# Second attention of a two-layer decoder: probabilities copied by transfers into float32r tiles, and transposed from there in three groups by query block

## The chip, the cores and the metric

The kernel runs on one core of one Trainium2 chip. The metric is the time of one execution in microseconds (us) on the device. TensorE (PE in the profile) multiplies and transposes, with its weight loads in a row of their own (PEld); VectorE is DVE, ScalarE is ACT, GpSimd is POOL; SP issues transfers and computes nothing.

## The reference

Two layers of a decoder on a sequence of 512 tokens with 1024 features. Layer 0 mixes tokens by stick-breaking attention, layer 1 by a sparse attention with 16 heads over a shared latent of 128; each is followed by a gated MLP. The change is in the sparse attention, the "second attention":

```python
def block(args):                       # one block of 128 queries
    ...
    _, sel = lax.top_k(isc, topk)      # an indexer picks 128 keys per query
    logits = jnp.einsum('bqhd,bqkd->bqhk', qb, kg) * scale
    logits = logits + jnp.swapaxes(bias, -1, -2).astype(jnp.float32)
    logits = jnp.where(valid[:, :, None, :], logits, NEG)
    p = jax.nn.softmax(logits, axis=-1)
    return jnp.einsum('bqhk,bqkd->bqhd', p, vg)
```

All arithmetic is in float32. The kernel computes the logits of all causal keys and adds a mask, so the 512 by 512 matrix of a head is cut into four query blocks `j` of 128 rows, block `j` having `(j + 1) * 128` keys: ten tiles of 128 by 128 per head.

## The kernel before, in words

Large products are made in three float32r products of a high and a low part (lines 694 to 696). In the second attention one loop runs over the heads `h`, and it is written as a software pipeline: while head `h` is transposed, head `n = h + 1` gets its logits and its softmax. The program order of each engine follows the written code; every engine, and the SP queue, takes its instructions in that order.

- `masked_bias(h, j)` writes the bias and the mask of a query block into a tile `L{j}` (two buffers for each `j`), by POOL for `j` below 2 and by ACT and POOL above (lines 2193 to 2205).
- `logits(n, j)` is three matmuls into a bank `z` (lines 1925 to 1927). `softmax(n, j)` adds the logits to the tile and finds the maximum, on DVE (line 1937). `expo(n, j)` makes the exponentials in place, with their sum, on ACT (line 2224). The division by the sum comes later, on the output.
- `transposed(h, pi, by_act)` turns the ten tiles of a head on PE, each by one transposing matmul with the identity into a PSUM bank `tr` (line 2234), in three groups `pi` of 4, 4 and 2, ordered by key block: group 0 holds key block 0 of all four query blocks, so it needs all four `expo` of the head. ACT copies group 0 out (line 2239), DVE groups 1 and 2 (line 2241), into a tile `pT`.
- `weighted(h)` multiplies `pT` of a pair of heads with the values, once in two heads, at the even ones (line 2265).
- `fill` puts in matmuls of other work: the last query projections (`pt_q`) and the first half of the output projection (`pt_o`), two, one or two lots per head at most.

In an iteration the order on PE is: `logits(n, 0)`, `logits(n, 1)`, at even `h` from 2 on `weighted(h - 2)`, group 0 of head `h`, `fill`, `logits(n, 2)`, group 1, `logits(n, 3)`, at odd `h` `pair_values`, group 2, `fill`. So between the logits of the third query block of a head and group 0 of the same head there stands one end of an iteration and one beginning.

The SP queue carries, in that stage, the bias rows `th` (line 1916), weights `raw` (line 613), and for each pair of heads the sums: `rvd` to memory (line 2276), and back, spread over the partitions, `bs` (line 2282, which waits until `rvd` has landed).

Of the kernel before, what the change touches and what calls it, by code (L numbers as in the profile page):

```python
# [9 lines left out]
F32 = mybir.dt.float32  # L10
F32R = mybir.dt.float32r
BF = mybir.dt.bfloat16
AF = mybir.ActivationFunctionType
OP = mybir.AluOpType
# [5 lines left out]
S = 512  # L20
P = 128
KT = D // P
QT = S // P
# [4 lines left out]
HEADS = 16  # L28
# [16 lines left out]
TRP = [[(0, 0)], [(1, 0), (3, 384)], [(2, 0)]]  # L45
TRW = [512, 512, 256]
LOFF = [0, 128, 384, 768]
LW = 1280
TRO = [0, 512, 1024]

C_ID, C_CAUSAL = 0, 128
C_W = 256
C_LEFT = LW - P
# [520 lines left out]
def kernel_body(ctx, tc, xT, wst, cst, smalls, crow, ccol, relb, outT):  # L574
    nc = tc.nc
    act, dve, pe, pool = nc.scalar, nc.vector, nc.tensor, nc.gpsimd

    cpool = ctx.enter_context(tc.tile_pool(name="cpool", bufs=1))
# [10 lines left out]
        return banks.tile(shape, F32, name=name, tag=tag, bufs=nbanks[tag])  # L589

    sm = cpool.tile([P, S_W], F32, name="sm")
    cons = cpool.tile([P, C_W], F32, name="cons")
    ident = cons[:, C_ID:C_ID + P]
    ones_r = cpool.tile([P, P], F32R, name="ones_r")
    ones_mean = ones_r.bitcast(F32)
    dve.memset(ones_mean, 1.0 / D)
# [355 lines left out]
    def stick_layer(l):  # L952
        with ExitStack() as st:
            man = ExitStack()
            man.enter_context(tc.manual_schedule())
            ap = st.enter_context(tc.tile_pool(name="att_a", bufs=2))
            head = ap.tile([P, 288], F32, name="head", tag="kz00", bufs=1)
            diag = ap.tile([P, LW], F32, name="diag", bufs=1)
# [211 lines left out]
            for k in range(3):  # L1170
                first_part(1, k)
            shift_dot(4)
            nc.sync.dma_start(cons, cst[:, C_LEFT:])
            load_ada(6)
            next(s4)
            fetch(5)
# [30 lines left out]
            for b in range(2):  # L1207
                for e in range(2):
                    pool.memset(kz[b][e][64 - 64 * e:128 - 64 * e].bitcast(F32), 0.0)
            mz = [ap.tile([P, LW], F32, name=f"mz{b}", bufs=1) for b in range(2)]  # L1210
            az = [ap.tile([P, LW], F32, name="a") for _ in range(2)]
            for b in range(2):
                for j in range(QT):
                    c = LOFF[j] + (j + 1) * P
# [599 lines left out]
    def dsa_layer(l, first, man):  # L1814
        with ExitStack() as st:
# [126 lines left out]
            with ExitStack() as si:  # L1942
# [22 lines left out]
                for j in range(1, QT):  # L1965
                    work[j] = ip.tile([P, (j + 1) * P], F32, name=f"work{j}")
                    pool.memset(work[j][:, :j * P], 0.0)
                    pool.tensor_copy(work[j][:, j * P:], cons[:, C_CAUSAL:C_CAUSAL + P])

                def lat_squares():  # L1970
                    ptl = ptile([P, S], "pt_latT", "tr")
# [54 lines left out]

                ptq = ptile([P, S], "pt_qi", "mm")
                drain(project_steps(ptq, chunk(("qi", 3), 0)))
                dve.tensor_scalar(maskb[:, :P], cons[:, C_CAUSAL:C_CAUSAL + P], -1.0, None, op0=OP.mult)
                ptw = ptile([P, S], "pt_w", "tr")  # L2030
                for j in range(QT):
                    pe.transpose(ptw[:, j * P:(j + 1) * P], kw[:, j * P:(j + 1) * P], ident)
# [89 lines left out]
            with ExitStack() as sa:  # L2122
# [70 lines left out]
                def masked_bias(h, j):  # L2193

                    ns = (j + 1) * P
                    c = h * QT + j
                    Ls[h, j] = ap.tile([P, ns], F32, name=f"L{j}")
                    L, b = Ls[h, j], ths[h][:, :ns][:, ::-1]
                    if h == 1:
                        dve.tensor_scalar(L, b, irq[:, c:c + 1], None, op0=OP.mult)  # L2200
                    elif h and j < 2:
                        pool.tensor_scalar(L, b, irq[:, c:c + 1], None, op0=OP.mult)
                    else:
                        act.activation(L, b, AF.Copy, scale=irq[:, c:c + 1])
                    pool.tensor_add(L, L, maskb[:, LOFF[j]:LOFF[j] + ns])
# [16 lines left out]
                def expo(h, j):  # L2222
                    nm, sum_ = heads[h][:2]
                    act.activation(Ls[h, j], Ls[h, j], AF.Exp, bias=nm[:, j:j + 1], scale=-1.0, accum_out=sum_[:, j:j + 1])

                trs = {}

                def transposed(h, pi, by_act):
                    tr = ptile([P, S], "tr", "tr")
                    w = TRW[pi]  # L2230
                    for i, c0 in TRP[pi]:
                        for j in range(i, QT):
                            c = c0 + (j - i) * P
                            pe.transpose(tr[:, c:c + P], Ls[h, j][:, i * P:(i + 1) * P], ident)  # L2234
                    if pi == 0:
                        trs[h] = ap.tile([P, LW], F32, name="pT", bufs=2)
                    t = trs[h][:, TRO[pi]:TRO[pi] + w]
                    if by_act:
                        act.activation(t, tr[:, :w], AF.Copy)
                    else:  # L2240
                        dve.tensor_copy(t, tr[:, :w])

                vals = {}

# [9 lines left out]
                def weighted(h):  # L2254

                    av = pair["av"] = ptile([P, S], "av", "mm")
                    ts = [trs.pop(h + e) for e in range(2)]
                    vs = vals.pop(h)
                    for pi in range(3):
                        for i, c0 in TRP[pi]:  # L2260
                            n = S - i * P
                            c = TRO[pi] + c0
                            for e in range(2):
                                hc = i * P + 64 * e
                                pe.matmul(av[64 * e:64 * e + 64, i * P:], lhsT=vs[:, hc:hc + 64],
                                          rhs=ts[e][:, c:c + n], start=i == 0, stop=pi == 2)

                def pair_sums(rv):
                    rvb = ap.tile([P, QT, 2, 64], F32, name="rvb", tag="bs")
# [47 lines left out]
                for j in range(QT):  # L2317
                    if j:
                        logits(0, j)
                    fill(1)  # L2320
                    if j:
                        softmax(0, j)
                    expo(0, j)
                    if j % 2 == 0:
                        masked_bias(1, j // 2)
                    if j == 0:
                        group_columns(2)
# [13 lines left out]
                for h in range(HEADS):  # L2341
                    n = h + 1
                    more = n < HEADS
                    values = h % 2 == 0 and h > 0
                    if more:
                        begin(n)
                        for j in range(2):
                            logits(n, j)
                        softmax(n, 0)
                        expo(n, 0)  # L2350
                    if values:
                        weighted(h - 2)
                    fill(LATE_STEPS[h][0])
                    transposed(h, 0, True)
                    if more:
                        softmax(n, 1)
                        expo(n, 1)
                        sums(h)
                    else:
                        rvb = sums(h)  # L2360
                        pair_values(h - 1)
                    follow(dve)
                    if h == 3:
                        q_newton(8, EARLY_Q)
                    if h == HEADS - 2:
                        late_dots(2)
                    if not more:
                        late_dots(1)
                    if h + 2 < HEADS:
                        masked_bias(h + 2, 0)  # L2370
                    fill(LATE_STEPS[h][1])
                    if h == 10:
                        follow(dve, 1)
                    if more:
                        logits(n, 2)
                        softmax(n, 2)
                        expo(n, 2)
                    transposed(h, 1, False)
                    if "row" in pair:
                        pair_rows()  # L2380
                    if h + 2 < HEADS:
                        masked_bias(h + 2, 1)
                    if h == 10:
                        follow(dve)
                    if more:
                        logits(n, 3)
                        softmax(n, 3)
                        expo(n, 3)
                    if h % 2 and more:
                        pair_values(h - 1)  # L2390
                    transposed(h, 2, False)
                    if h + 2 < HEADS:
                        for j in range(2, QT):
                            masked_bias(h + 2, j)
                    if n + 3 < HEADS:
                        load_bias(n + 3)
                    if h == 1:
                        q_seed(8, EARLY_Q)
                    if values:
                        pair_hi()  # L2400
                    elif h > 1:
                        pair_lo()
                    fill(LATE_STEPS[h][2])
                    follow(act)
                    if h == HEADS - 4:
                        load_dots(3)
                        bias_job(2, "col")
                    if h == 7:
                        follow(dve)
                    if not more:  # L2410
                        pair_scale(rvb)
# [140 lines left out]
```

## Time and profile before

| what | value |
|---|---|
| time, median of the runs | 1212.46 us |
| the profiled execution: time | 1212.47 us |
| the profiled execution: span of the core | 1210.7 us |
| time around the span | 1.8 us |
| second attention, first to last transpose of line 2234 | 723.7 to about 834 us |

The span is the time from the first to the last instruction on the core. In the rows below a timeline row gives start, duration, engine, line, operation, output and inputs with their shapes; "x4" says that four like instructions were merged in one row. In the rows of transfers the last number is the median time from issue to landing. A tile's buffer numbers are left out.

### The profile page before, as it was taken

To read this page: it belongs to the slowest core of one execution; us is meant where nothing else is said; L and a number is where in the kernel's file an instruction comes from. 1 tells how busy PE (TensorE), PEld (TensorE's weight loads), DVE (VectorE), ACT (ScalarE), POOL (GpSimd) and SP (SyncE) were. 2 spreads that over 40 slices of the span, in tenths; PEclk is the share of its full clock that TensorE was granted. 3 is DMA by queue.
4 is the path that set the end of the run, shared out by engine and by line. 5 is a ranking of instruction groups with operands and counts; after the bars stand their busy time and mean duration, and the time that the engine had idled before them with its cause. 6 is when DMAs were issued, how large, how long until landed. Compare 5 with 4: busy or idle time off the path is not lost.

```text
span 1210.7 us, 18277 instructions
## 1 busy us (share of the span) xinstructions
PE 1204.2 (99%) x6532; PEld 1009.1 (83%) x6532; DVE 1024.2 (85%) x1736; ACT 800.0 (66%) x1366; POOL 243.5 (20%) x282
## 2 busy tenths in 40 slices
PE   9999999999999999999999999999999999999998
PEld 6888788788898998998888777777888888888887
DVE  5898888998989988999788995668989898889883
ACT  5588787368666676765657357774786677677660
POOL 0001100001111111211000357784012122112110
PEclk9999999999999999999999999999999999999999
DMA  9778897629789898896520242245499888788662
GB/s 377 249 205 231 224 244 240 209 87 220 192 217 277 230 245 217 225 290 174 183 70 18 70 140 57 84 137 167 137 234 212 225 190 204 182 184 190 155 147 87
DMA packets 79923, 224.89 MB, mean 186 GB/s; under 512 B 16588, under 2 KB 17356, under 8 KB 79832
## 3 DMA queue, kind: packets, MB, share of 16 engines
q1 hardware_dynamic: 59616, 169.16, 42.3%
q0 software_dynamic: 20192, 54.54, 25.5%
q8 instruction: 51, 0.84, 0.3%
q14 instruction: 40, 0.33, 0.1%
q10 hardware_dynamic: 24, 0.02, 0.0%
HBM read 212.62 MB, written 2.16 MB: 177 GB/s over the span
## 4 chain that ended last, share of the span: by engine, by line
PE 98%; DMA 1%; ACT 0%; DVE 0%; issue 0%; SPq 0%
PE pt_d L1741 16%; PE pt_a L1653 8%; PE pt_u L1622 6%; PE pt_a L1649 6%; PE pt_d L1653 4%; PE pt_u L1626 3%; PE pt_d L1649 3%; PE pt_q L694 2%; PE pt_q L696 2%; PE pt_l L694 2%; PE pt_q L695 2%; PE pt_l L695 2%; PE pt_l L696 2%; PE pt_qk L694 2%; PE pt_qk L696 2%; PE pt_qk L695 2%
## 5 line engine op out<-in xcount | busy, mean ns | idle before, releaser
L1741 PE MATMUL pt_d<-actlo,dnhi 128*128 128x512 f32 x288 | 112.8, 392 | 0.0
L1741 PE MATMUL pt_d<-acthi,dnhi 128*128 128x512 f32 x288 | 112.8, 392 | 0.0
L1531 ACT ACTIVATE whi<-raw 128x1024 fp32r<-128x1024 f32 x72 | 75.8, 1054 | 29.6 <-PE pt_a L1653 13.1
L644 ACT ACTIVATE whi<-raw 128x1024 fp32r<-128x1024 f32 x80 | 84.2, 1052 | 3.6 <-issue 1.1
L1622 PE MATMUL pt_u<-hh,whi 128*128 128x512 f32 x320 | 75.8, 389 | 0.0
L1741 PE MATMUL pt_d<-acthi,dnlo 128*128 128x512 f32 x288 | 73.5, 391 | 0.0
L662 POOL DMA_DIRECT2D wlo<-wst x23 | 19.9, 866 | 265.2 <-DVE hh L806 114.1
L1622 PEld LDWEIGHTS pt_u<-hh,whi 128*128 128x128 f32 x320 | 60.0, 188 | 12.6 <-issue 0.2
L1543 POOL DMA_DIRECT2D wlo<-wst x37 | 32.0, 865 | 167.1 <-ACT wlo L1539 91.4
L1741 PEld LDWEIGHTS pt_d<-actlo,dnhi 128*128 128x128 f32 x288 | 54.3, 188 | 10.1
L1741 PEld LDWEIGHTS pt_d<-acthi,dnhi 128*128 128x128 f32 x288 | 54.2, 188 | 10.1
L1741 PEld LDWEIGHTS pt_d<-acthi,dnlo 128*128 128x128 f32 x288 | 53.1, 188 | 10.3
L653 POOL TENSOR_TENSOR wlo<-raw,whi 128x1024 fp32r<-128x1024 f32 x18 | 44.2, 2456 | 85.7 <-PE pt_q L695 45.8
L1649 PE MATMUL pt_a<-hh,whi 128*128 128x512 f32 x228 | 61.3, 391 | 0.0
L1349 DVE TENSOR_TENSOR_SCAN mz<-mz,diag 128x768 f32<-128x768 f32 (+1 forms) x32 | 47.6, 1487 | 15.2 <-ACT mz L1343 15.0
L722 DVE SCALAR_TENSOR_TENSOR raw<-raw,cond 128x1024 f32<-128x1024 f32 x46 | 57.3, 1273 | 1.4 <-ACT cond L1167 1.3
L1653 PE MATMUL pt_a<-hh,wlo 128*128 128x256 f32 x360 | 57.4, 282 | 0.0
L1653 PEld LDWEIGHTS pt_a<-hh,wlo 128*128 128x128 f32 x360 | 53.1, 190 | 4.5
L1937 DVE CUSTOM_DVE_ANT_0 L<-z,L,cols 128x128 f32<-128x128 f32 (+3 forms) x60 | 32.3, 546 | 28.7 <-PE tr L2234 20.7
L1554 POOL DMA_DIRECT2D whi<-wst x30 | 26.0, 866 | 132.8 <-ACT whi L1551 82.6
L694 PE MATMUL pt_q<-hh,whi 128*128 128x512 f32 x128 | 51.8, 405 | 0.0
L722 DVE SCALAR_TENSOR_TENSOR ada<-ada,cond 128x1024 f32<-128x1024 f32 x41 | 50.0, 1219 | 1.7 <-DMA ada<-wst 1.7
(409 smaller groups left out, 3803.3 us busy)
## 6 DMA issues: line engine op xcount, KB each, us to landing
raw<-wst SPq DMA_DIRECT2D x215, 512.0 KB, 5.2
wlo<-wst POOLq DMA_DIRECT2D x60, 512.0 KB, 7.8
ada<-wst SPq DMA_DIRECT2D x45, 512.0 KB, 5.4
raw<-wst SPq DMA_DIRECT2D x48, 384.0 KB, 4.8
whi<-wst POOLq DMA_DIRECT2D x30, 256.0 KB, 5.8
dnlo<-wst POOLq DMA_DIRECT2D x16, 384.0 KB, 7.0
x<-xt POOLq DMA_DIRECT2D x18, 256.0 KB, 5.6
th<-relb SPq DMA_DIRECT2D x16, 256.0 KB, 4.0
```

Of the source, the lines that this page charges most:

```text
L644: act.activation(hi[:, :n], raw[:, :n], AF.Copy)
L653: engine.tensor_sub(lo[:, :w], raw[:, :w], hi[:, :w].bitcast(F32))
L694: pe.matmul(out, lhsT=whi, rhs=ahi, start=start, stop=False)
L695: pe.matmul(out, lhsT=wlo, rhs=ahi, start=False, stop=False)
L696: pe.matmul(out, lhsT=whi, rhs=alo, start=False, stop=stop)
L722: dve.scalar_tensor_tensor(raw, raw, 1.0, cond, op0=OP.mult, op1=OP.mult, accum_out=dst)
L1349: dve.tensor_tensor_scan(rev, rev, diag[:, b:e][:, ::-1], 0.0, OP.mult, OP.max)
L1531: act.activation(W[j, i][0], R[j, i], AF.Copy)
L1622: pe.matmul(pt[j, i], lhsT=W[j, i][0][:, k * P:(k + 1) * P], rhs=hs[k][n], start=k + n == 0, stop=False)
L1649: pe.matmul(pt[j, bank, "both"], lhsT=w[:, c0 + k * P:c0 + (k + 1) * P], rhs=a[2], start=new and k == 0, stop=False, skip_group_check=True)
L1653: pe.matmul(out, lhsT=w[:, c0 + k * P:c0 + (k + 1) * P], rhs=a[n], start=new and k + n == 0, stop=part == 1 and k == 3 and what in ("a2", ...
L1741: pe.matmul(pt["dn", i], lhsT=dn[i][part][:, k * P:(k + 1) * P], rhs=A[j0 + k][n], start=part + k + n == 0, stop=part == 1 and k == j1 - j ...
```

## The change

For heads 0 to 14, a transfer on the SP queue copies the exponentials into tiles `ra` (query blocks 0 to 2, 768 columns) and `rb` (query block 3, 512 columns), one buffer each, which are of type float32r; the bytes are copied as they are. The tiles `L0`, `L1`, `L2` become one tile `La`, so that one transfer moves three query blocks (head 0 is moved in four pieces). PE transposes from the copies, as float32r with a float32r identity. The groups are now by query block: the first two take three tiles each of query blocks 0 to 2, the third the four tiles of query block 3. `pT` is written in strided slots, and `weighted` reads it so. Head 15 is transposed from its own tiles as before, in the new groups. The identity is made once by POOL from `diag`, and serves all float32 transposes through a view of the same bytes; `cons` keeps the causal mask only.

```diff
+SLOTS = [slice(0, 7, 2), slice(3, 8, 2), slice(1, 9, 7), slice(9, 10)]
+TURNS = [([(0, 0), (0, 1), (0, 2)], slice(0, 5, 2)), ([(2, 2), (1, 1), (1, 2)], slice(1, 6, 2)),
+         ([(0, 3), (1, 3), (2, 3), (3, 3)], slice(6, 10))]
...
-    ident = cons[:, C_ID:C_ID + P]
+    ident_r = cpool.tile([P, P], F32R, name="ident_r")
+    ident = ident_r.bitcast(F32)
...
+            pool.tensor_copy(ident_r, diag[:, :P])
...
-                    Ls[h, j] = ap.tile([P, ns], F32, name=f"L{j}")
+                    if j == 0:
+                        Ls[h] = ap.tile([P, LOFF[3]], F32, name="La")
+                    Ls[h, j] = Ls[h][:, LOFF[j]:LOFF[j] + ns] if j < 3 else ap.tile([P, ns], F32, name="Lb")
...
+                def move(h, js):
+                    for j in js:
+                        if j == 0:
+                            moved[h, 0] = ap.tile([P, LOFF[3]], F32R, name="ra", bufs=1)
+                        if j == 3:
+                            moved[h, 1] = ap.tile([P, S], F32R, name="rb", bufs=1)
+                    if h and 0 in js:
+                        nc.sync.dma_start(moved[h, 0].bitcast(F32), Ls[h])
+                    elif h:
+                        nc.sync.dma_start(moved[h, 1].bitcast(F32), Ls[h, 3])
...
-                    for i, c0 in TRP[pi]:
-                        for j in range(i, QT):
-                            c = c0 + (j - i) * P
-                            pe.transpose(tr[:, c:c + P], Ls[h, j][:, i * P:(i + 1) * P], ident)
+                    blocks, slots = TURNS[pi]
+                    for n, (i, j) in enumerate(blocks):
+                        c, k = slice(n * P, n * P + P), slice(i * P, i * P + P)
+                        if h == HEADS - 1:
+                            pe.transpose(tr[:, c], Ls[h, j][:, k], ident)
+                        else:
+                            src = moved[h, 1] if j == 3 else moved[h, 0][:, LOFF[j]:]
+                            pe.transpose(tr[:, c].bitcast(F32R), src[:, k], ident_r)
...
                     transposed(h, 1, False)
+                    if n < HEADS - 1:
+                        move(n, [0, 1, 2])
...
                     transposed(h, 2, False)
+                    if n < HEADS - 1:
+                        move(n, [3])
```

Three places show how the instructions stand. First the SP queue around heads 3 and 4; `th` is a bias row, `rvd` and `bs` the sums out and back, `raw` a chunk of weights. Before:

```order
L1916 DMA th<-relb 128x512 x2
L2276 DMA rvd<-rv 128x2x4
L2282 DMA bs<-rvd 64x512 x2
L1916 DMA th<-relb 128x512
L613 DMA raw<-wst 128x1024
```

And with the change, over the same stretch:

```order
L1921 DMA th<-relb 128x512
L2245 DMA ra<-La 128x768
L2247 DMA rb<-Lb 128x512
L1921 DMA th<-relb 128x512
L2302 DMA rvd<-rv 128x2x4
L2245 DMA ra<-La 128x768
L2308 DMA bs<-rvd 64x512 x2
L2247 DMA rb<-Lb 128x512
L1921 DMA th<-relb 128x512
L617 DMA raw<-wst 128x1024
```

At head 3 the two copies stand between two bias rows; at head 4 the copy `ra` stands ahead of the transfer `bs`, and `rb` behind it. The second place is the SP queue in the iteration of heads 12 and 13, where three chunks of weights stand (`shd` is a small row for a later bias). Before:

```order
L1916 DMA th<-relb 128x512
L613 DMA raw<-wst 128x1024 x3
L710 DMA shd_8460<-mod_88 128x8
L2276 DMA rvd<-rv 128x2x4
L2282 DMA bs<-rvd 64x512 x2
L613 DMA raw<-wst 128x1024 x3
```

And with the change:

```order
L1921 DMA th<-relb 128x512
L2245 DMA ra<-La 128x768
L2247 DMA rb<-Lb 128x512
L617 DMA raw<-wst 128x1024 x3
L714 DMA shd_8492<-mod_89 128x8
L2302 DMA rvd<-rv 128x2x4
L2245 DMA ra<-La 128x768
L2308 DMA bs<-rvd 64x512 x2
L2247 DMA rb<-Lb 128x512
L617 DMA raw<-wst 128x1024 x3
```

The three chunks, which followed the bias row, now stand behind the two copies of head 13. The third place is PE, from the last matmul of the logits of head 3's third query block (width 384) on; the transposes here are those of head 2. Before:

```order
L1927 MATMUL z<-kpl,qh 128x384
L2234 MATMUL tr<-cons,L_7363 128x128
L2234 MATMUL tr<-cons,L_7376 128x128
L2234 MATMUL tr<-cons,L_7379 128x128 x2
L1925 MATMUL z<-kph,qh 128x512
L1926 MATMUL z<-kph,ql 128x512
L1927 MATMUL z<-kpl,qh 128x512
L2234 MATMUL tr<-cons,L_7376 128x128
L2234 MATMUL tr<-cons,L_7379 128x128
L694 MATMUL pt_q<-hh,whi 128x512
```

And with the change:

```order
L1932 MATMUL z<-kpl,qh 128x384
L2263 MATMUL tr<-ident_r,ra 128x128 x3
L1930 MATMUL z<-kph,qh 128x512
L1931 MATMUL z<-kph,ql 128x512
L1932 MATMUL z<-kpl,qh 128x512
L2263 MATMUL tr<-ident_r,rb 128x128 x4
L698 MATMUL pt_q<-hh,whi 128x512
```

The order of the work on PE stays; six transposes in this stretch became seven, and the last four now read `rb`.

More of the change, by code (lines that the diff above doesn't have):

```diff
@@ L591, in kernel_body @@
     sm = cpool.tile([P, S_W], F32, name="sm")
-    cons = cpool.tile([P, C_W], F32, name="cons")
-    ident = cons[:, C_ID:C_ID + P]
+    cons = cpool.tile([P, P], F32, name="cons")
+    ident_r = cpool.tile([P, P], F32R, name="ident_r")
+    ident = ident_r.bitcast(F32)
     ones_r = cpool.tile([P, P], F32R, name="ones_r")
@@ L1172, in stick_layer @@
             shift_dot(4)
-            nc.sync.dma_start(cons, cst[:, C_LEFT:])
+            nc.sync.dma_start(cons, cst[:, C_LEFT + C_CAUSAL:])
             load_ada(6)
@@ L1967, in dsa_layer @@
                     pool.memset(work[j][:, :j * P], 0.0)
-                    pool.tensor_copy(work[j][:, j * P:], cons[:, C_CAUSAL:C_CAUSAL + P])
+                    pool.tensor_copy(work[j][:, j * P:], cons)
                 def lat_squares():
@@ L2028, in dsa_layer @@
                 drain(project_steps(ptq, chunk(("qi", 3), 0)))
-                dve.tensor_scalar(maskb[:, :P], cons[:, C_CAUSAL:C_CAUSAL + P], -1.0, None, op0=OP.mult)
+                dve.tensor_scalar(maskb[:, :P], cons, -1.0, None, op0=OP.mult)
                 ptw = ptile([P, S], "pt_w", "tr")
@@ L2226, in dsa_layer @@
                 trs = {}
+                moved = {}
+                def move(h, js):
[9 more added lines that the diff above has]
+                    else:
+                        for j in js:
+                            ns = (j + 1) * P
+                            to = moved[h, 1] if j == 3 else moved[h, 0][:, LOFF[j]:LOFF[j] + ns]
+                            nc.sync.dma_start(to.bitcast(F32), Ls[h, j])
@@ L2228, in transposed @@
                 def transposed(h, pi, by_act):
                     tr = ptile([P, S], "tr", "tr")
-                    w = TRW[pi]
-                    for i, c0 in TRP[pi]:
-                        for j in range(i, QT):
-                            c = c0 + (j - i) * P
-                            pe.transpose(tr[:, c:c + P], Ls[h, j][:, i * P:(i + 1) * P], ident)
+                    blocks, slots = TURNS[pi]
[3 more added lines that the diff above has]
+                            pe.transpose(tr[:, c], Ls[h, j][:, k], ident)
+                        else:
+                            src = moved[h, 1] if j == 3 else moved[h, 0][:, LOFF[j]:]
+                            pe.transpose(tr[:, c].bitcast(F32R), src[:, k], ident_r)
@@ L2235, in transposed @@
                     if pi == 0:
-                        trs[h] = ap.tile([P, LW], F32, name="pT", bufs=2)
-                    t = trs[h][:, TRO[pi]:TRO[pi] + w]
+                        trs[h] = ap.tile([P, LW], F32, name="pT", bufs=2).rearrange("p (s c) -> p s c", c=P)
+                    t, v = trs[h][:, slots], tr[:, :len(blocks) * P].rearrange("p (s c) -> p s c", c=P)
                     if by_act:
-                        act.activation(t, tr[:, :w], AF.Copy)
+                        act.activation(t, v, AF.Copy)
@@ L2240, in transposed @@
                     else:
-                        dve.tensor_copy(t, tr[:, :w])
+                        dve.tensor_copy(t, v)
                 vals = {}
@@ L2258, in weighted @@
                     vs = vals.pop(h)
[L2259 to L2266, printed above, removed]
+                    for i in (0, 1, 3, 2):
+                        for e in range(2):
+                            hc = i * P + 64 * e
+                            pe.matmul(av[64 * e:64 * e + 64, i * P:].rearrange("p (s c) -> p s c", c=P), lhsT=vs[:, hc:hc + 64],
+                                      rhs=ts[e][:, SLOTS[i]], start=i == 0, stop=i == 2)
                 def pair_sums(rv):
@@ L2323, in dsa_layer @@
                     expo(0, j)
+                    move(0, [j])
                     if j % 2 == 0:
```

## The prediction

> **What bounds the kernel now.** I read the page first, for the engine that sets the end, then the stretches of the second attention, then PE's waits there, and last the timeline of single heads.
>
> ```profile
> span 1210.7 us, 18277 instructions
> PE 1204.2 (99%) x6532; PEld 1009.1 (83%) x6532; DVE 1024.2 (85%) x1736; ACT 800.0 (66%) x1366; POOL 243.5 (20%) x282
> PE 98%; DMA 1%; ACT 0%; DVE 0%; issue 0%; SPq 0%
> sum 120.00, PE 118.81 PEld 94.15 DVE 82.37 ACT 84.58 POOL 87.84; mean PE 9.90 PEld 7.85 DVE 6.86 ACT 7.05 POOL 7.32
> PE av L2265 <- ACT vals L2252: 0.7, 1, 0.7
> PE z L1925 <- DVE nm L1937: 0.4, 1, 0.4
> ```
>
> The second row is the busy time by engine, the third the chain that ended last, the fourth the sum over twelve stretches of 10 us from 720 to 840 us, the last two are all waits that PE has from 720 to 840 us. PE is busy for 1204.2 of 1210.7 us and makes 98% of the chain; in the second attention it is busy for 118.81 of 120 us and waits for others for 1.1 us. So what makes PE's own work in this stage shorter comes off the end, and every new wait of PE is added to it. DVE, ACT and POOL have 32 to 38 us of idle time there. PE takes its work in order, so a transpose that waits holds up all that stands behind it, `fill` too.
>
> **What the transposes cost.** The timeline of PE at group 1 of head 2, and at two narrow logits a little later:
>
> ```profile
> 741.06 0.60 PE L2234 MATMUL tr<-cons,L 128*128 128x128 f32 x4
> 741.42 0.48 PE L1925 MATMUL z<-kph,qh 128*128 128x512 f32 x1
> 741.74 0.39 PE L1926 MATMUL z<-kph,ql 128*128 128x512 f32 x1
> 741.97 0.40 PE L1927 MATMUL z<-kpl,qh 128*128 128x512 f32 x1
> ...
> 743.81 0.22 PE L1925 MATMUL z<-kph,qh 128*128 128x128 f32 x1
> 743.87 0.27 PE L1926 MATMUL z<-kph,ql 128*128 128x128 f32 x1
> 743.98 0.28 PE L1927 MATMUL z<-kpl,qh 128*128 128x128 f32 x1
> 744.09 0.33 PE L1925 MATMUL z<-kph,qh 128*128 128x256 f32 x1
> ```
>
> Durations overlap, so I go by starts. From 741.06 to 741.74 PE does four float32 transposes and one matmul of 512 columns; the next one of 512 columns takes 741.97 - 741.74 = 0.23. The four cost 0.68 - 0.23 = 0.45, that is 0.112 us each. What would a float32r operation of this size cost? The logits of lines 1925 to 1927 are float32r, and at 128 columns the steps are 0.06, 0.11 and 0.11: the first has its weights loaded ahead under a longer matmul, and each one that follows with new weights takes 0.11. A transpose has new weights every time (the probabilities are the stationary operand), so I expect a float32r transpose to step by 0.11 too, as a float32 one does. **150 transposes at 0.112 become 150 at about 0.11: 0 us.** Bounds: at 0.06, if the weights were no limit, 150 x 0.052 = 7.8 us less; on the other side 0.113, the longest such step that I see, nothing that counts. I take 0, since two of the three steps in these rows say so.
>
> A rule of the Trainium skill says otherwise. "TensorE: Matmul & The Clock Gate", section "Weight-path perf modes — Fast Weight Load (FWL) and DoubleRow", has weights of 128 columns loaded faster, about twofold as measured there, when their type is not FP32. If float32r counts as such, the new transposes would come at the lower bound, and the sum would be that of the first rival below. The 0.11 steps of the float32r logits speak against it here.
>
> **What the copies add.** Before, PE reads the exponentials as soon as ACT has made them. Now a transfer stands between, and group 0 of head `n` needs query blocks 0 to 2 of that head. So the gap counts between the end of `expo(n, 2)` on ACT and the first transpose of head `n` on PE, as it is now. Heads in order (each pair: the exponentials of 384 columns, then the first transposes of the same head): 0, 1, 4, 7, 9, 12, 13.
>
> ```profile
> 721.77 0.62 ACT L2224 ACTIVATE Lu<-Lu,cols 128x384 f32<-128x384 f32 x1
> 723.69 0.49 PE L2234 MATMUL tr<-cons,Lu 128*128 128x128 f32 x3
> ...
> 727.13 0.62 ACT L2224 ACTIVATE L<-L,nm 128x384 f32<-128x384 f32 x1 [0.57 <-DVE nm L1937]
> 729.60 0.38 PE L2234 MATMUL tr<-cons,L 128*128 128x128 f32 x2
> ...
> 749.60 0.62 ACT L2224 ACTIVATE L<-L,nm 128x384 f32<-128x384 f32 x1 [0.28 <-DVE nm L1937]
> 754.53 0.33 PE L2234 MATMUL tr<-cons,L 128*128 128x128 f32 x1
> ...
> 771.50 0.62 ACT L2224 ACTIVATE L<-L,nm 128x384 f32<-128x384 f32 x1 [0.91 <-DVE nm L1937]
> 773.28 0.49 PE L2234 MATMUL tr<-cons,L 128*128 128x128 f32 x3
> ...
> 784.48 0.62 ACT L2224 ACTIVATE L<-L,nm 128x384 f32<-128x384 f32 x1 [0.92 <-DVE nm L1937]
> 787.45 0.38 PE L2234 MATMUL tr<-cons,L 128*128 128x128 f32 x2
> ...
> 805.70 0.60 ACT L2224 ACTIVATE L<-L,nm 128x384 f32<-128x384 f32 x1
> 810.00 0.33 PE L2234 MATMUL tr<-cons,L 128*128 128x128 f32 x1
> ...
> 813.39 0.62 ACT L2224 ACTIVATE L<-L,nm 128x384 f32<-128x384 f32 x1 [1.60 <-DVE nm L1937]
> 815.85 0.38 PE L2234 MATMUL tr<-cons,L 128*128 128x128 f32 x2
> ```
>
> Start plus duration of the first row, taken from the start of the second, gives the gap. The odd heads are short: 1.85 at head 1 and 1.84 at head 13, the first and the last of five alike (1, 3, 5, 11, 13); 1.16 at head 7, 2.35 at head 9. The even heads have `weighted` ahead of group 0 and are long: 4.31 at head 4, and the shortest is 3.70 at head 12. Head 0 has 1.30. The new groups add one transpose to the stretch (six became seven), so each gap from head 1 on grows by 0.1.
>
> How long a copy takes no row shows: none here goes from SBUF to SBUF on the SP queue. The nearest rows are these (KB each, median from issue to landing):
>
> ```profile
> raw<-wst SPq DMA_DIRECT2D x48, 384.0 KB, 4.8
> th<-relb SPq DMA_DIRECT2D x16, 256.0 KB, 4.0
> bs<-rvd SPq DMA_DIRECT2D x14, 128.0 KB, 2.9
> outT<-x SPq DMA_DIRECT2D x6, 256.0 KB, 2.0
> outT<-x SPq DMA_DIRECT2D x4, 128.0 KB, 1.7
> ```
>
> `ra` has 384 KB. Read from SBUF as `outT` is, it takes 2.0 + 0.3 = 2.3 (0.3 for another 128 KB); as the loads from memory do, up to 4.8. At 128 KB the transfer that writes SBUF, `bs`, takes 1.2 more than the one that reads it; how much of that is the write, I can't tell. I take 2.8, nearer to `outT`, and keep 2.3 and 4.8 as the ends. To it come 0.1 for ACT to read out its sum before it signals, and 0.1 for PE to start anew (both estimates from the tenth or so between neighbours in these rows): **the first transpose can start 3.0 us after the exponentials.** The Trainium skill, "DMA: Bandwidth & Descriptors", section "Anatomy of one DMA — SWDGE (gpsimd) path", has 2.0 us plus bytes over 436 GB/s; by that `ra` takes 2.9, an estimate, and the sum would be 0.8 us longer. No run so far shows such a copy.
>
> The waits of PE, 3.0 less the gap: heads 1, 3, 5, 11, 13 at 3.0 - 1.95 = 1.05 make 5.25; head 7 at 3.0 - 1.26 makes 1.74; head 9 at 3.0 - 2.45 makes 0.55; head 0, whose last piece is 192 KB (0.45 less than 384 KB, so 2.55 in all), 2.55 - 1.30 = 1.25. The even heads from 2 on have at least 3.8 and wait for nothing. **Sum 8.8 us.** Behind the waiting transpose stand the logits of the next head and `fill`, so nothing covers it; after it everything moves on by the same amount, and the gaps stay as they are, because the way from a logit through DVE and ACT follows PE.
>
> **What I cost at nothing, and what covers it.** `rb` is read by group 2 of its head, a whole iteration of PE's work after it is issued, which hides it; if that were gone, PE would wait for it as for `ra`. The copy-outs of the groups are 3, 3 and 4 tiles, not 4, 4 and 2: the same bytes on ACT and DVE, which have the idle time above. `weighted` has the same sixteen matmuls in another order. `La` comes free when `ra` has landed, which is no later than the transposes that freed `L` before. POOL's copy of the identity falls in a long idle time before the first transposes.
>
> **The SP queue.** It is in order, so a copy waits there for ACT, and what stands behind it waits along.
>
> ```profile
> 810.46 1.38 SPq L613 DMA_DIRECT2D raw<-wst  x3
> ```
>
> The three chunks left at 810.46, ahead of the exponentials of head 13 (done at 814.01); now they stand behind both its copies and leave some 5 us later. Then `rvd`, `ra` of head 14 and `bs` follow close behind 1.5 MB. `bs` waits for `rvd` to land, and `rb` of head 14 stands behind `bs`. Head 14 has a long gap, so I take 0, with 1 us as the upper bound. In the earlier iterations each chunk follows a bias row that already waits for ACT, so it keeps its place.
>
> **Sum:** 1210.7 + 1.8 around the span + 0 + 8.8 = 1221.3, so 1221. The profiled run, 1212.47, and the median, 1212.46, are the same number.
>
> **The rivals.**
>
> *The transposes become cheaper and pay for the waits* (not slower). With 0.06 each, PE saves 7.8; but seven of them lie in the gap, which shrinks by 0.36 at seven odd heads, so 2.5 come back. With my copy: 8.8 + 2.5 - 7.8 = 3.5, time 1216; with a copy of 2.3: 4.8 + 2.5 - 7.8 = -0.5, time 1212. For it speaks the step of 0.06 where weights are loaded ahead; against it, that a row of transposes never has that. The rule on fast weight loads named above (the Trainium skill, "TensorE: Matmul & The Clock Gate") would bring it about. Chance 0.17.
>
> *The copy is as slow as a load* (slower by over 2%). At 4.8 the first transpose starts 5.0 after the exponentials: each of the eight heads waits 2.0 longer than above, 24.8 in all, and the even heads wait too, 1.2 at head 12, 0.6 at head 4 and likewise at two or three more, about 3: time 1240. The point from which this decides is a copy of about 4.5 us, since 2% is 24 us (about what a measurement of this kernel can tell from no change). For it speaks that `raw` and `th` take 4.0 and more; against it, that these read memory and often stand behind others in the queue, while the copies mostly go out alone. Chance 0.07; for a copy from 3.5 to 4.5, which gives 1227 to 1236, another 0.13.
>
> *The copies are hidden after all.* With a landing under 1.7 us only head 7 would wait: time 1213. The shortest row, 1.7 for a third of the bytes, speaks against it. Chance 0.05.
>
> **How the numbers follow.** My forecast (transposes as before, a copy of 2.3 to 3.5, so 1217 to 1227) has 0.58. The range from 1212 to 1233 takes in the rival with cheaper transposes, and most of the slow copies; what is left out is the copy of over 4.2 us (0.1) and a few cases below. Faster by over 2% needs 24 us, more than all the transposes cost (150 x 0.112 = 16.8): 0.01. Slower by over 2%: 0.07. Within: 0.92.
>
> **What the profile after would show.** A new wait of PE at the float32r transposes, put down to the transfers of `ra`, at heads 0 and the odd ones, about 1 us each, and none or little at the even ones. Starts of three transposes 0.11 apart. `ra` from issue to landing about 2.8. No other stage changes. I am wrong if the steps are near 0.06, if the landing is over 4 us, if PE waits at `rb`, or if DVE or ACT become what PE waits for.

## The result, and the profile after

The changed kernel takes 1225.56 us (median; 1225.11 to 1226.19) where the kernel before took 1212.45 beside it: a ratio of 1.0109, with an interval of 1.0089 to 1.0128. It is slower by 13.1 us, which is inside the 2% that counts as no change and inside the range, 4.6 us above the predicted 1221. One of the four runs of the kernel before took 2427.06 us, far from the other three, and the ratio goes without it. The profiled execution took 1225.82 us, with a span of 1224.0 against 1210.7; the 13.3 us between the spans are what has to be explained.

From the page and from the view of transfers of the changed kernel: the span, the busy times, the chain, and the two copies (KB, median from issue to landing).

```profile
span 1224.0 us, 18401 instructions
PE 1206.2 (99%) x6532; PEld 1007.8 (82%) x6532; DVE 1026.6 (84%) x1736; ACT 799.2 (65%) x1366; POOL 243.6 (20%) x283
PE 91%; DMA 2%; DVE 2%; ACT 1%; POOL 1%; issue 1%; SPq 0%; DVEq 0%; POOLq 0%; ACTq 0%
ra<-La SPq DMA_DIRECT2D x14, 384.0 KB, 2.9
rb<-Lb SPq DMA_DIRECT2D x14, 256.0 KB, 2.6
```

PE's busy time grew by 2 us, the span by 13: most of the time is in waits. The chain, which was PE for 98%, now goes over transfers (2%), DVE (2%), ACT and POOL as well. PE's waits from 715 to 855 us, by releaser (total, times, longest); a last one, for a maximum, is 0.3:

```profile
PE tr L2263 <- DMA ra<-La: 8.2, 8, 1.6
PE av L2291 <- DVE pT L2270: 1.8, 1, 1.8
PE tr L2263 <- DMA ra<-Lu: 1.6, 2, 1.2
```

The first and the third row are the wait that was forecast: 9.8 us at the transposes, for the copies into `ra`. Of these 1.2 are at head 10, where none was forecast. There is none for `rb`. The second row, a wait of `weighted(14)` for DVE, was not forecast.

**The gap between exponentials and transposes.** For heads 1, 3 and 4 the exponentials of 384 columns, and the first transposes of the same head:

```profile
729.89 0.62 ACT L2231 ACTIVATE La<-La,nm 128x384 f32<-128x384 f32 x1 [1.77 <-DVE nm L1942]
733.34 0.42 PE L2263 MATMUL tr<-ident_r,ra 128*128 128x128 f32 x3 [0.84 <-DMA ra<-La]
745.53 0.61 ACT L2231 ACTIVATE La<-La,nm 128x384 f32<-128x384 f32 x1 [1.78 <-DVE nm L1942]
749.25 0.43 PE L2263 MATMUL tr<-ident_r,ra 128*128 128x128 f32 x3 [1.13 <-DMA ra<-La]
752.95 0.62 ACT L2231 ACTIVATE La<-La,nm 128x384 f32<-128x384 f32 x1 [0.28 <-DVE nm L1942]
758.21 0.44 PE L2263 MATMUL tr<-ident_r,ra 128*128 128x128 f32 x3
```

Head 1: 733.34 - 730.51 = 2.83. Head 3: 749.25 - 746.14 = 3.11. The other odd heads lie between 2.83 and 2.89. Head 4 has 4.64 and no wait in brackets: the copy is there long before `weighted(2)` is done.

**The transposes.** PE at groups 1 and 2 of head 2:

```profile
744.56 0.38 PE L2263 MATMUL tr<-ident_r,ra 128*128 128x128 f32 x3
744.77 0.46 PE L1930 MATMUL z<-kph,qh 128*128 128x512 f32 x1
745.07 0.39 PE L1931 MATMUL z<-kph,ql 128*128 128x512 f32 x1
...
745.53 0.46 PE L2263 MATMUL tr<-ident_r,rb 128*128 128x128 f32 x4
745.83 0.47 PE L698 MATMUL pt_q<-hh,whi 128*128 128x512 f32 x1
746.13 0.40 PE L699 MATMUL pt_q<-hh,wlo 128*128 128x512 f32 x1
```

By the method of the prediction (start of the group to start of the second matmul behind it, less 0.23): (745.07 - 744.56 - 0.23) / 3 = 0.093, and (746.13 - 745.53 - 0.23) / 4 = 0.093 for a float32r transpose, against 0.112 for a float32 one. 150 of them save 150 x 0.019 = 2.9 us.

**Where the 13.3 us went.** I compared the starts of PE's matmuls in the two traces, which stand in the same order but for a few places. A step in the difference is what was lost there (a minus is a gain); it is a little more than the wait in brackets, since without a wait a matmul starts ahead of the end of the one before it.

| part | forecast, us | in the trace, us |
|---|---|---|
| waits for `ra`, heads 1, 3, 5, 7, 9, 11, 13 | 7.5 | 1.02 + 1.30 + 1.38 + 1.75 + 0.57 + 1.10 + 1.03 = 8.15 |
| waits for `ra`, head 0 | 1.25 | 2.2 |
| wait for `ra`, head 10 | 0 | 1.15 |
| 150 transposes | 0 | -2.9 |
| PE at half clock behind the wait of head 7 | not seen | +1.5 |
| last head: DVE late with `pT` | not seen | +2.8 |
| head 4: the kernel before waits 0.7 for its values at `weighted(2)`, the changed one does not | not seen | -0.8 |
| ahead of the stage, nearly all in a step at 483 us | not seen | +0.8 |
| behind the stage, at 1079 us | not seen | +0.4 |
| sum | 8.8 | 13.3 |

The change does not touch the code at 483 and at 1079 us. Experiment 2, which has no copies, loses 1.1 us at the first of these places, and experiment 7, which has them, nothing at either, so these steps do not come from the copies. The wait at head 4 is gone in experiment 2 as well.

**The half clock.** A view of two neighbouring stretches (busy time of PE, PEld, DVE, ACT, POOL with counts, then the granted clock, the share of the DMA engines, GB/s):

```profile
776.45:779.86 3.41, 1.83 (x15) 1.52 (x13) 3.07 (x10) 2.98 (x8) 3.24 (x6) 1.00 0.58 226
779.86:783.27 3.41, 3.41 (x13) 2.92 (x12) 0.73 (x3) 1.24 (x6) 3.24 (x5) 0.50 0.51 85
```

In the first, PE waits for head 7 and is busy for 1.83 of 3.41 us. In the second it has no gap, but the clock is 0.50: PE gets through thirteen instructions, where experiment 6 has 24 at the same place at full clock. So at most half of the 3.41 us is lost, 1.7; the starts of PE's matmuls on the two sides of the stretch move apart by 1.5 against experiment 6.

**The last head.** The wait for `pT`, in the changed kernel:

```profile
844.84 2.35 POOL L657 TENSOR_TENSOR wlo<-raw,whi 128x1024 fp32r<-128x1024 f32 x1 [6.91 <-ACT whi L648]
844.92 2.29 DVE L730 TENSOR_TENSOR mod<-mod,sm 128x8 f32<-128x8 f32 x1
847.13 1.14 DVE L2270 COPY pT<-tr 128x384 f32<-128x384 f32 x2
848.33 1.94 PE L2291 MATMUL av<-pT,vals 128*64 128x512 f32 x12 [1.75 <-DVE pT L2270]
```

And the same two operations in the kernel before:

```profile
834.57 0.17 DVE L726 TENSOR_TENSOR mod<-mod,sm 128x8 f32<-128x8 f32 x1
834.60 2.38 POOL L653 TENSOR_TENSOR wlo<-raw,whi 128x1024 fp32r<-128x1024 f32 x1 [6.90 <-ACT whi L644]
```

DVE's addition to `mod`, eight columns wide, takes 0.17 us where it starts 0.03 ahead of POOL's large operation on `wlo`, and 2.29 us, until that operation has ended (847.21 and 847.19), where it starts 0.08 behind it. The copies to `pT` stand behind it on DVE, and `weighted(14)` waits for them. PE's matmuls just ahead of `weighted(14)` start 10.2 us later than in the kernel before, those just behind it 13.0, so the last head costs 2.8, more than the 1.75 in brackets.

### The profile page after: what moved, and what is told of

It reads as the page before. It is cut to its first block, busy times and chain, and to the rows that moved or that the text cites. A ratio compares the mean times of both kernels' runs of the same rounds, so it can differ in the third digit from the quotient of the medians.

```text
span 1224.0 us, 18401 instructions
## 1 busy us (share of the span) xinstructions
PE 1206.2 (99%) x6532; PEld 1007.8 (82%) x6532; DVE 1026.6 (84%) x1736; ACT 799.2 (65%) x1366; POOL 243.6 (20%) x283
## 4 chain that ended last, share of the span: by engine, by line
PE 91%; DMA 2%; DVE 2%; ACT 1%; POOL 1%; issue 1%; SPq 0%; DVEq 0%; POOLq 0%; ACTq 0%
PE pt_d L1746 16%; PE pt_a L1658 8%; PE pt_u L1627 6%; PE pt_a L1654 5%; PE pt_d L1658 4%; PE pt_u L1631 3%; PE pt_d L1654 3%; PE pt_l L698 2%; PE pt_l L700 2%; PE pt_l L699 2%; PE pt_qk L698 2%; PE pt_q L698 2%; PE pt_qk L700 2%; PE pt_qk L699 2%; PE pt_q L700 2%; PE pt_q L699 2%
## 5 line engine op out<-in xcount | busy, mean ns | idle before, releaser
L1746 PEld LDWEIGHTS pt_d<-actlo,dnhi 128*128 128x128 f32 x288 | 54.2, 188 | 10.2
L1942 DVE CUSTOM_DVE_ANT_0 La<-z,La,cols 128x128 f32<-128x128 f32 (+2 forms) x45 | 21.1, 481 | 35.1 <-PE z L1932 27.6
```

The costliest lines, as they stand in the source:

```text
L1746: pe.matmul(pt["dn", i], lhsT=dn[i][part][:, k * P:(k + 1) * P], rhs=A[j0 + k][n], start=part + k + n == 0, stop=part == 1 and k == j1 - j ...
```

## Experiments

The theories carry one name each below, beside the letters of the quoted expectations. **Waits:** PE stands still until `ra` has landed, and all else moves on with it. **Clock:** a wait can bring a stretch at half clock. **Tail:** the wait for `pT` is an accident of order between DVE and POOL. The rivals are that the new groups, the strided copies or the extra load on the queue cost the time. The ratios below go by runs of the kernel before that were taken beside each experiment; their medians, 1213.05 us for experiments 1 to 4 and 1212.99 for 5 to 8, lie some 0.6 above the 1212.45 beside the changed kernel, so a difference between two of the times below can be off by about as much.

**1. Copies, but all in float32.** `ra`, `rb` and the transposes are float32; the order is that of the change.

```diff
-    moved[h, 0] = ap.tile([P, LOFF[3]], F32R, name="ra", bufs=1)
+    moved[h, 0] = ap.tile([P, LOFF[3]], F32, name="ra", bufs=1)
...
-    pe.transpose(tr[:, c].bitcast(F32R), src[:, k], ident_r)
+    pe.transpose(tr[:, c], src[:, k], ident)
```

> The kernel with the change, but the copies and their transposes are float32 (same transfers, same groups). Theory A (a float32r transpose steps by 0.093 us, a float32 one by 0.112; the copies' waits are the cost): 150 x 0.019 = 2.9 us more work on PE, of which about 1.1 comes back because the seven transposes in the gap make the waits shorter: about 1227.4 us, waits for ra about 8.5 us. Rival B (the type makes no difference, as the prediction had it): 1225.6 us, waits for ra as with the change, about 9.8 us.

Measured: 1224.38 us (1224.05 to 1225.59), ratio 1.0095 (1.008 to 1.011), span 1222.5. Both expectations are missed on the low side: I had set them out from the time of the changed kernel, and in this run neither the wait for `pT` nor the half clock came. PE's waits for copies:

```profile
PE tr L2263 <- DMA ra<-La: 8.2, 8, 2.0
PE tr L2263 <- DMA ra<-Lu: 1.8, 3, 1.3
```

In all they are again about 10 us, so it is not the type of the copies that makes PE wait. In detail they differ: head 10 alone waits 1.96 here and 1.20 in the changed kernel, and without it the waits are 8.0 against 8.6, which goes the way of theory A, whose slower transposes lengthen the gap. At the last head DVE's addition started at 845.92, 0.04 ahead of POOL's operation, and took 0.17 us again.

**2. The groups alone.** No copies; float32 transposes from `La` and `Lb`, in the new groups and slots.

```diff
-    if h == HEADS - 1:
+    if True:
         pe.transpose(tr[:, c], Ls[h, j][:, k], ident)
...
-    if n < HEADS - 1:
-        move(n, [0, 1, 2])
```

> The kernel with the change without its transfers: float32 transposes straight from La and Lb, in the new groups, with the strided pT. Theory A (the waits for the copies are the cost): no wait of PE at the transposes; what stays is the end of the stage, where weighted waits for DVE's last copy-outs of head 15, 2.3 us: about 1214.8 us. Rival C (the new groups or the strided slots cost it): 1220 us or more. If the late copy-outs are an accident of the copies' timing: 1212.5 us.

Measured: 1211.88 us (1211.38 to 1212.59), ratio 0.9991 (0.9981 to 1.0), span 1210.8. PE's only wait from 715 to 855 us:

```profile
PE z L1930 <- DVE nm L1942: 0.2, 1, 0.2
```

The groups by query block, the strided copies to `pT` and the joined tile `La` cost nothing. Between this kernel and the one of experiment 1 only the copies differ. The times are 12.5 us apart; the starts of PE's matmuls in the two traces part by 11.7, all of it at head 0, the odd heads and head 10, and 10.0 of that are the waits in brackets.

**3. float32r without copies.** ACT writes the exponentials straight into the float32r tiles, in place of having their bytes copied; nothing is moved, and all 160 transposes are float32r. `Lb` and `rb` have one buffer each.

```diff
-    act.activation(Ls[h, j], Ls[h, j], AF.Exp, bias=nm[:, j:j + 1], scale=-1.0, accum_out=sum_[:, j:j + 1])
...
+    to = Rs[h, 1] if j == 3 else Rs[h][:, LOFF[j]:LOFF[j] + (j + 1) * P]
+    act.activation(to, Ls[h, j], AF.Exp, bias=nm[:, j:j + 1], scale=-1.0, accum_out=sum_[:, j:j + 1])
```

> No transfers: ACT writes the exponentials straight into float32r tiles (they are rounded to float32r there, which is the part of the computation that is changed), and all 160 transposes are float32r. One buffer instead of two for Lb and rb. Theory A: 160 x 0.019 = 3.0 us less than the kernel with the groups only: 1211.8 us with the wait at the end of the stage, 1209.5 us without it. Rival B (the type makes no difference): the same time as the kernel with the groups only.

Measured: 1214.63 us (1213.36 to 1217.19), ratio 1.0013 (1.0004 to 1.0022), span 1213.8. The waits for copies are gone, but the kernel is not faster than before. From 720 to 828 us PE gained 2.3 us on the kernel before; then came the wait for `pT`:

```profile
PE av L2276 <- DVE pT L2255: 2.2, 1, 2.2
```

```profile
833.40 2.34 POOL L657 TENSOR_TENSOR wlo<-raw,whi 128x1024 fp32r<-128x1024 f32 x1 [6.91 <-ACT whi L648]
833.49 2.28 DVE L730 TENSOR_TENSOR mod<-mod,sm 128x8 f32<-128x8 f32 x1
```

POOL started 0.09 ahead, DVE's addition took 2.28 us, and behind the wait the clock was at one half from 838.05 on for 3.41 us. So the wait for `pT` does not need the copies. With the half clock it costs 4.8 us here, by the starts of PE's matmuls against experiment 5. Experiment 5 takes it away.

**4. The `fill` ahead of group 0.** Copies as in the change, but at head 0 and the odd heads the matmuls of `fill` that stood behind group 0 go ahead of it, so that PE has work while the copy lands.

```diff
+LATE_STEPS = [(a + b, 0, c) if h % 2 and h < 15 or h == 0 else (a, b, c) for h, (a, b, c) in enumerate(LATE_STEPS)]
```

> The kernel with the change, but at head 0 and the odd heads up to 13 the one or two lots of other matmuls that stood behind group 0 stand ahead of it, which adds 1.4 us (0.7 at head 7) to the gap between the exponentials and group 0. Theory A: with a copy of 2.9 us the waits go at all heads except head 7 (1.0 us left) and head 10 (1.1 us, whose copy stands behind a chunk of weights), and with the wait of 1.6 us at head 7 the stretch of 3.4 us at half the granted clock: 1225.6 - 7.7 - 1.7 - 1.5 (starting anew) = about 1214.7 us. Rival D (PE only waits elsewhere, as the logits that follow are not later but the copies are): 1220 us or more.

Measured: 1217.38 us (1216.42 to 1217.85), ratio 1.0035 (1.0022 to 1.0048), span 1216.1. The first and the second wait in the trace:

```profile
PE tr L2264 <- DMA ra<-La: 1.9, 2, 1.0
PE av L2292 <- DVE pT L2271: 1.7, 1, 1.7
```

8.2 us at eight places became 1.9 at two, and the kernel came out 8.2 us faster than the changed one. The transfers themselves are all still there, so it is PE's standing still that costs, and not the load on the queue. The time is 2.7 above what the first theory gave; the wait for `pT`, again 1.7, and smaller ones for `rb` and for the values, which it left out, are most of that.

**5. As 3, with the last head mended.** At the last head DVE's additions to `mod` (`late_dots(1)`) go behind its copies to `pT`.

```diff
-                    if not more:
-                        late_dots(1)
...
                     transposed(h, 2, False)
+                    if not more:
+                        late_dots(1)
```

> ACT writes the exponentials (rounded to float32r) straight into float32r tiles, no copies; and at the last head DVE's copies to pT stand ahead of its small additions to mod, so that these additions no longer stand between POOL's wlo and pT. The same without the second part took 1214.6, with a wait for pT of 2.2 us and a stretch of 3.4 us at half clock behind it. Theory T (the wait for pT comes from an addition that stalls beside POOL, and the wait brings the half clock): wait for pT gone, no half clock there, 1214.6 - 2.2 - 1.7 = 1210.7 or a little less, 1209.5 to 1211, which is 1 to 3 us under the kernel before. Theory U (float32r exponentials make that wait, whatever the order on DVE): the wait for pT stays above 1.5 us and the time is 1214 to 1215.

Measured: 1210.85 us (1210.65 to 1213.05), ratio 0.9981 (0.9972 to 0.999), span 1208.9. All waits of PE from 715 to 855 us, and the last head:

```profile
PE av L2276 <- ACT vals L2266: 1.0, 2, 0.8
PE z L1930 <- DVE nm L1942: 0.3, 1, 0.3
```

```profile
832.64 3.33 POOL L657 TENSOR_TENSOR wlo<-raw,whi 128x1024 fp32r<-128x1024 f32 x1 [6.92 <-ACT whi L648]
831.47 1.15 DVE L2255 COPY pT<-tr 128x384 f32<-128x384 f32 x2
833.78 2.21 DVE L730 TENSOR_TENSOR mod<-mod,sm 128x8 f32<-128x8 f32 x1
```

The addition still starts inside POOL's operation and still lasts until its end, but nothing that PE needs is behind it. The medians of experiments 3 and 5 lie 3.8 us apart, where 2.2 + 1.7 = 3.9 were expected. That they agree so well is partly luck: the runs of experiment 3 go from 1213.36 to 1217.19, with mean clocks from 0.998 to 1.0, and the two profiled runs are 4.9 apart. This is the version that beats both kernels, by 2.1 us the one before; that is a difference that this measurement shows, though far under 2%. Experiment 2, which has no float32r transposes, is already 1.2 under the runs of before beside it.

**6. The changed kernel with the last head mended.** The same edit on the changed kernel.

> The changed kernel with DVE's copies to pT of the last head ahead of the small additions; the copies by transfers stay. Theory T: the wait for pT (1.8) goes, nothing else changes: 1225.6 - 2.0 = 1223.6, 1223 to 1224.2 where head 7 still brings 3.4 us at half clock, and 1.7 less where it does not. Theory U (the tail's wait belongs to the later arrival of the whole stage and comes back at another place): 1225 to 1226.

Measured: 1224.77 us (1223.3 to 1226.57), ratio 1.0096 (1.0082 to 1.011), span of the profiled run 1222.3. The wait for `pT` is gone from the trace, and the span is 1.7 shorter, though the waits for copies came to 11.3 us here against 9.8 (head 10 waited 2.06). The median moved only by 0.8 and its spread overlaps that of the changed kernel, so by the time alone this stays inconclusive. The spread goes with the clock: the four runs had mean clocks of 0.999 (1223.3 us), 0.998 (1224.1) and 0.997 (1225.44, 1226.57). The profiled run shows where the clock fell, and where not. Two pairs of neighbouring stretches, first around head 7, then around head 0:

```profile
777.67:781.08 3.41, 1.81 (x15) 1.50 (x13) 3.33 (x10) 2.98 (x8) 3.24 (x6) 1.00 0.59 230
781.08:784.50 3.42, 3.42 (x24) 3.11 (x24) 1.55 (x4) 2.13 (x8) 3.25 (x5) 1.00 0.54 114
...
723.06:726.47 3.41, 1.68 (x10) 1.13 (x8) 2.93 (x10) 1.31 (x4) 2.40 (x4) 1.00 0.80 144
726.47:729.88 3.41, 3.01 (x9) 2.35 (x9) 0.00 (x0) 0.98 (x3) 2.58 (x4) 0.50 0.56 155
```

The wait at head 7, 1.6 us again, was followed by full clock here (24 instructions in the stretch behind it, where the changed kernel had 13); the first two of the three waits of head 0, 1.7 us, which fell into one stretch, were followed by half.

**7. Experiment 4 with the last head mended.**

> Copies by transfers, the fill ahead of group 0 at head 0 and the odd heads (1217.4 as run), and DVE's copies to pT of the last head ahead of the small additions. Theory T: 1217.4 - 2.0 = 1215.4, 1214.8 to 1216. Theory U: 1217 to 1218. If it is at 1215.4, the waits that are left (about 5 us) and not the copies as such are all that the change still costs.

Measured: 1215.23 us (1214.46 to 1216.45), ratio 1.0017 (1.0008 to 1.0027), span 1213.5: the first theory's number within 0.2. The wait for `pT` is gone, and 3.9 us of waits for copies are left; 1.0 for the values comes beside them, as in experiment 5:

```profile
PE tr L2264 <- DMA ra<-La: 2.6, 3, 1.3
PE tr L2264 <- DMA ra<-Lu: 0.9, 2, 0.6
PE tr L2264 <- DMA rb<-Lb: 0.4, 1, 0.4
```

It is 4.4 us slower than experiment 5, whose transposes wait for no copy.

**8. Every copy into `ra` twice.** For heads 1 to 14; the second waits for the first.

```diff
                         nc.sync.dma_start(moved[h, 0].bitcast(F32), Ls[h])
+                        nc.sync.dma_start(moved[h, 0].bitcast(F32), Ls[h])
```

> The changed kernel with the transfer into ra made twice in a row for heads 1 to 14; the second waits for the first, so ra is there about 2.9 later. Theory A (PE waits for the copy, in full, and all that is behind it moves on): the seven odd heads wait 2.9 more each (20.3), the even ones, whose gap is 3.8 to 4.4 against 5.9 now, 1.5 to 2.1 each (about 12): 1225.6 + 32 = 1258, 1250 to 1262 without a clock effect. Theory C (every wait of about 1.6 us or more of PE brings 3.4 us at half clock): another 1.7 for each of some 13 waits, so 1275 to 1285. Theory H (the second transfer lies beside the first, or the waits are hidden by the order): under 1240.

Measured: 1262.77 us (1261.43 and 1264.1), ratio 1.0408 (1.0389 to 1.0427), span 1262.3, mean clock 0.985. The copies and PE's waits for them:

```profile
ra<-La SPq DMA_DIRECT2D x28, 384.0 KB, 2.6
PE tr L2264 <- DMA ra<-La: 34.4, 12, 5.4
```

With 2.0 at head 0 the waits grew from 9.8 to 36.4 us; that is 26.6 of the 38.3 us between the spans, and theory A's 32 was somewhat too much. The other 11.7 us are put down to the clock, as what is left over: it was at one half for eleven times 3.41 us, where the changed kernel had one such stretch. PE was busy for 33.9 us in the eleven, so they can have cost up to 16.9; how much of that moved the end was not measured apart. Heads 1 and 3:

```profile
731.72:735.13 3.41, 0.34 (x3) 0.14 (x2) 1.63 (x6) 2.15 (x6) 2.03 (x2) 1.00 0.53 205
735.13:738.54 3.41, 2.99 (x9) 2.53 (x10) 0.00 (x0) 0.98 (x3) 2.61 (x4) 0.50 0.49 136
...
752.20:755.61 3.41, 0.09 (x1) 0.00 (x0) 2.16 (x11) 2.42 (x6) 2.02 (x2) 1.00 0.45 171
755.61:759.02 3.41, 2.90 (x9) 2.44 (x10) 0.32 (x2) 1.08 (x4) 2.61 (x4) 0.50 0.48 142
```

Theory C, with 1.7 us for each of thirteen waits, gave too much as well: not every wait brings a stretch at half clock, and PE waits during some of them, where a slow clock costs nothing.

## Why the prediction was right, and where its steps were off

- **The waits for the copies** carry the result, as forecast. The landing of `ra`, taken as 2.8 between bounds of 2.3 and 4.8, is 2.9; the gap, taken as 3.0, is 2.83 to 3.11; the odd heads lose 8.15 us for a forecast of 7.5, and heads 7 and 9 come out at 1.75 and 0.57 for 1.74 and 0.55. The agreement is not as close everywhere: heads 3 and 5 come out at 1.30 and 1.38 for 1.05 each. The even heads wait for nothing but at head 10, and `rb` nowhere. Experiment 2 shows that without the copies nothing is lost, experiment 4 that work put under the copies takes most of the waits away, experiment 8 that a later landing is paid for. The Trainium skill, "DMA: Bandwidth & Descriptors", section "Anatomy of one DMA — SWDGE (gpsimd) path", has 2.0 us plus bytes over 436 GB/s for transfers that GpSimd issues; by that `ra` takes 2.9 and `rb` 2.6 (estimates). The copies here were issued by SP, and their medians are 2.9 and 2.6.
- **Head 0** was costed as one copy of 192 KB behind the last exponentials. Its three pieces go out one behind another, and SP does not issue them as fast as ACT makes them:

```profile
L2252 SPq DMA_DIRECT2D ra<-Lu x3: 547/552/1419, 721.8 to 724.5; - x3
```

  (shortest, median and longest issue in ns, first and last start.) One issue took 1.42 us, and the third piece went out at 724.5, 1.3 behind its exponentials. So it lost 2.2 instead of 1.25.
- **The SP queue** was costed at nothing, with the reason that chunks of weights keep their place in the earlier iterations. They do, but a copy of the next head now stands close behind one, with only `rvd` between them:

```profile
795.43 0.43 SPq L617 DMA_DIRECT2D raw<-wst  x1
795.96 0.38 SPq L2302 DMA_DIRECT2D rvd<-rv  x1
799.36 0.47 SPq L2245 DMA_DIRECT2D ra<-La  x1
804.69 0.42 PE L2263 MATMUL tr<-ident_r,ra 128*128 128x128 f32 x3 [1.20 <-DMA ra<-La]
```

  The copy for head 10 landed 5.2 us after its issue, where the median is 2.9, and an even head waited. Head 10 waited again in experiments 1 and 6, for 1.96 and 2.06 us. That it shared the DMA engines with the 384 to 512 KB of the chunk is likely, but no run took the chunk away.
- **The transposes** are the term that was mis-sized: 0 us forecast, -2.9 in the trace. I took the step of float32r logits with new weights, 0.11, for that of a transpose; it is 0.093. The lower bound of 0.06 is not seen either. The prediction tied it to the rule on fast weight loads (the Trainium skill, "TensorE: Matmul & The Clock Gate", section "Weight-path perf modes — Fast Weight Load (FWL) and DoubleRow"), by which weights that are not FP32 load about twice as fast.
- **"No other stage changes"** failed at the last head: 2.8 us. It is also one of the prediction's own signs of being wrong, that DVE becomes what PE waits for. The copies out of PSUM were costed at nothing because DVE is idle for 38 us of the stage, which is an average: at this place one held-up operation stood ahead of them. The order of DVE's instructions there is the old one; what changed is who starts first, by 0.1 us. Experiments 5, 6 and 7 take the wait away by the order alone, and experiments 1 and 2 do not have it, since DVE happens to come first in them.
- **The half clock** was no term at all. It took 1.5 us in the changed kernel and some 12 in experiment 8, there as what is left over.
- **The rivals.** That the transposes pay for the waits is out: they pay 2.9 of 11.5. A copy as slow as a load is out, but for head 10. That a gain of 2% was all but ruled out was right, for the reason given: even without copies the kernel with float32r transposes is only 2.1 us faster than the one before (experiment 5).

The forecast missed by 4.6 us, and its parts by more: -2.9 for the transposes and -0.8 at head 4 stand against +2.8 and +1.5 that I had not seen, +2.1 at heads 0 and 10, +0.7 at the odd heads and 1.2 outside the stage, which no run explains. So the mechanism was right and the waits of the odd heads were well sized; that the whole came within 4.6 us is partly luck, since gains of 3.7 hide losses of 8.3 that were not in the sum.

## What to carry to other kernels

On an engine that never waits, a detour through a transfer costs its landing less the slack between the last producer and the first consumer, place by place; that sum is read from the trace of before, and moving other work into the gap takes most of it back. Look first whether the engine that makes the data can write it in the wanted type, which here does away with the copy. When a change shifts a stage by a few us, look at what stands close together in time on other engines further on: an order that was decided by 0.03 us can turn over and cost more than the change's own terms.

## What the runs showed of the hardware that was not expected

- **PE's clock** fell to one half for 3.41 us after a stretch of 3.41 us in which PE was busy for 1.83, 1.68, 0.34 or 0.09 us. It did not after 1.81 us in experiment 6, nor after 1.87 in the changed kernel (844.71 to 848.13, the wait for `pT`), nor after 1.70 at the end of experiment 8 (1257.37 to 1260.78). So the busy time that a profile shows, with its modelled ends of matmuls, does not settle by itself where the clock falls: between 1.68 and 1.83 us it went both ways. The starts of the half stretches in experiment 8 (735.13, 755.61, 769.27, 779.51) lie 6, 4 and 3 times 3.413 apart, so the stretches lie on a fixed grid there. That a wait which is split between two stretches goes free fits the wait of 1.96 us in experiment 1, from 803.46 on, across the border at 804.98: PE was busy for 1.88 and 2.97 us in the two, and the clock stayed full. No run shifted one wait against the grid to show it. The Trainium skill, "TensorE: Matmul & The Clock Gate", Part 1, has a free-running window of about 3.4 us, which these starts agree with, and lets the clock fall after at least one idle window; here PE was still busy for half of one.
- **DVE beside POOL:** an addition of 128 by 8 took 2.21 to 2.29 us where it started 0.08 us or more behind a POOL operation of 128 by 1024 with operands in SBUF, and 0.17 where it started 0.01 to 0.04 ahead of it (the kernel before, experiments 1 and 2). It ended 0.02 to 0.03 behind POOL's operation in each case (the changed kernel, experiments 3, 4 and 5).
- **A float32r transpose** of 128 by 128 steps by 0.093 us in a row of three or four, a float32 one by 0.112.
